# Four RWKV pairs in one tick: corrections and outputs share one PSUM bank, state products have another

## The chip, the cores and the metric

The kernel runs on one core of one Trainium2 chip. The metric is device microseconds (us) for one launch, taken as the median over runs. An engine is one of PE (matmul), DVE (vector), ACT (scalar), POOL (GpSimd) and SP (which issues most DMAs); each works through its own queue in order.

## The reference

One hybrid layer is computed for 256 context tokens and 1024 latent tokens. A combined input projection feeds a differential attention (8 heads) and a bidirectional RWKV-7 recurrence (16 heads of size 64), and an output projection joins both. What the change touches is the recurrence, the attention that is woven into it, and the order of both:

```python
def step(S, inp):                       # rwkv_scan, per token, per head, two directions
    r_t, w_t, k_t, v_t, kk_t, b_t = inp
    sa = jnp.einsum('bhvk,bhk->bhv', S, -kk_t)
    S = S * w_t[:, :, None, :] + sa[..., None] * b_t[:, :, None, :] + v_t[..., None] * k_t[:, :, None, :]
    return S, jnp.einsum('bhvk,bhk->bhv', S, r_t)
...
s = jnp.einsum('bqhmd,bkhmd->bhmqk', qblk, k).astype(F32) * scale      # diff_attention, per 128 queries
p = jax.nn.softmax(s, axis=-1)
a = p[:, :, 0] - lam * p[:, :, 1]
return jnp.einsum('bhqk,bkhv->bqhv', a.astype(v.dtype), v)
```

## The kernel before

The first stage (to about 1249 us) is the input projection and the preparation of the recurrence's operands in DRAM. The second stage, `mix_phase`, runs the recurrence, the attention, the norms and most of the output projection together. The rest is a tail with the last attention blocks and the last set of the output projection.

**The recurrence.** Heads come in pairs; four pairs (`NL = 4`) go side by side as two "duos" (`w` 0 and 1, `e` the pair in it, `h` the head, `d` the direction). Tokens are cut into segments of 256 and chunks of 32. An item is one segment of one group of four pairs; there are ten items (`m`), five for each group. A **tick** (`t`, 80 in all, eight to an item) is one chunk, and `step` writes its work out. In a tick PE makes 16 small matmuls of *corrections* (line 893), which ACT copies out for duo 0 and DVE for duo 1 (line 901, four copies each) into rows 96:128 of the operand tile `R`. Then come 16 matmuls of *state products* (line 913), which DVE multiplies by decays into the next chunk's `R` (line 924, four operations), and 16 matmuls of *outputs* (line 936), which ACT copies to `ys` (line 939, one copy for each duo). `L` and `R` have two slots for each duo, one for a "part" of two chunks; `load_part` fetches the part after next, and `prep` (line 803) multiplies it by the inverse.

**PSUM.** `bank[w]` holds all three products of duo `w`: corrections in columns 0:128, outputs in 128:256, state products in 256:512. All instructions that touch one such tile are ordered by the framework by its bank, not by its columns.

**The attention.** `attention()` is a generator of 80 blocks of 128 queries: scores (`sc`, line 1057, two PSUM buffers), their eviction with a running minimum (line 1060, DVE), exponentials (line 1068, ACT), the combination of both maps (line 1081, DVE), transposes (`pa`, line 1089, copied by ACT in line 1091) and values (`po`, line 1104). `fill` is called twice in a tick, once between corrections and state products and once after the outputs. It adds to a `credit` and draws pieces of attention until that is spent: 1.06 of an even share in the first 40 ticks, 0.68 in the others. What is left goes to the tail. `fill` also moves on the norms of finished items (line 980 and after), the output projection (lines 1255 on) and `invert`.

**The inverse.** For each item but the first, POOL computes 128 triangular 32x32 inverses in 31 steps (two operations each, lines 734 and 736). 16 DMAs bring the matrices (`aw`, line 726), one takes the result to DRAM (line 738), and `load_inv` fetches it for each part. `invert(m + 1)` is begun in the first tick of item `m`, and moved on by eight steps in a tick.

**What sets the order.** PE's queue is the order in which the program is written. On the other engines a list scheduler with a modelled timeline places the instructions; `ahead(500)` around lines 901 and 924 raises their priority.

Of the kernel before, what the change touches and what calls it, by code (L numbers as in the profile page):

```python
# [10 lines left out]
F32 = mybir.dt.float32  # L11
# [7 lines left out]
P = 128  # L19
# [13 lines left out]
CH = 32  # L33
SEG = 256
NC = SEG // CH
HN = 2
NF = NC // HN
NL = 4
# [702 lines left out]
def mix_phase(ctx, tc, i, o, s, ident, nhalf, dram, td0, neglam, subg, lnh, heads, psm):  # L741
    nc = tc.nc
# [85 lines left out]
    def invert(b):  # L828
        rows = inv_rows(heads, b)
        aw = wk.tile([P, CH, CH], F32, tag="aw", name=f"aw{b}")  # L830
        tt = wk.tile([P, CH, CH], F32, tag="tt", name=f"tt{b}")
        tmp = wk.tile([P, CH * CH // 4], F32, tag="tmp", name=f"tmp{b}")
        tds[b] = dram.tile([CH, P, CH], F32, tag=f"td{b % 2}", name=f"td{b}")
        yield from inverse(nc, s, tds[b], rows, aw, tt, tmp)

    bank = [psx.tile([P, 512], F32, name=f"bank{w}") for w in duos]
    yb = psx.tile([P, 512], F32, name="yb")
    sts, wcs = {}, {}

# [15 lines left out]
    def start_item(w, m):  # L855
        p0, sg = items[m]
        R = slots[w, 0][1]
        if sg == -1:
            nc.gpsimd.memset(R[0:64, 0], 0.0)
        if sg != 0:  # L860
            return
        px = bank[w]
        turned = lambda v: v.rearrange("p (d v) -> p d v", d=2)
        for e in range(2):
            p = p0 + 2 * w + e
            for g in range(4):
                c = slice(64 * (g % 2), 64 * (g % 2) + 64)
                nc.tensor.transpose(px[0:64, 64 * g:64 * g + 64], R[0:64, 0, g // 2, e, c], ident[0:64, 0:64])
                nc.tensor.transpose(px[0:64, 256 + 64 * g:256 + 64 * g + 64], sts[p][:, g // 2, c], ident[0:64, 0:64])
            nc.scalar.copy(R[0:64, 0, :, e], turned(px[0:64, 256:512]))  # L870
            fo = wk.tile([HD, 2, P], F32, tag="st", name=f"fo{p}", bufs=NL)
            nc.scalar.copy(fo, turned(px[0:64, 0:256]))
            for d in range(2):
                nc.sync.dma_start(o["new_s"][0, 0, d, 2 * p:2 * p + 2].rearrange("h v k -> v h k"),
                                  fo[:, d, :].rearrange("v (h k) -> v h k", h=2))

    ysb = {}
# [4 lines left out]
    def step(j, k, fill):  # L882
        m, f = j // NF, j % NF
        c = HN * f + k
        p0, sg = items[m]
        hv = lambda h: slice(64 * h, 64 * h + 64)
        for w in duos:
            L, R = slots[w, j % 2]
            for d in range(2):
                for e in range(2):  # L890
                    for h in range(2):
                        u = 64 * e + 32 * h
                        nc.tensor.matmul(bank[w][u:u + 32, 64 * d:64 * d + 64], L[0:96, e, h, d, k, 96:128],
                                         R[0:96, k, d, e, hv(h)], start=True, stop=True, tile_position=(0, u))
        with ahead(HPC):
            for w in duos:
                R = slots[w, j % 2][1]
                for e in range(2):
                    for h in range(2):
                        u = 64 * e + 32 * h  # L900
                        (nc.vector.tensor_copy if w else nc.scalar.copy)(
                            R[96:128, k, :, e, hv(h)], bank[w][u:u + 32, 0:128].rearrange("p (d v) -> p d v", d=2))
        later_prep = k == HN - 1 and j + 1 < n_part
        if later_prep:
            prep(j + 1, 0, yb)
        fill(0)
        for w in duos:
            L, R = slots[w, j % 2]
            for e in range(2):
                for d in range(2):  # L910
                    for h in range(2):
                        o_ = 256 + 128 * d + 64 * e
                        nc.tensor.matmul(bank[w][hv(h), o_:o_ + 64], L[:, e, h, d, k, 0:64],  # L913
                                         R[:, k, d, e, hv(h)], start=True, stop=True, tile_position=(0, 64 * h))
        with ahead(HPC):
            for w in duos:
                if k < HN - 1:
                    dst = slots[w, j % 2][1][0:64, k + 1]
                elif f == NF - 1 and sg == 3:
                    continue  # L920
                else:
                    dst = slots[w, (j + 1) % 2][1][0:64, 0]
                for h in range(2):
                    nc.vector.tensor_tensor(dst[:, :, :, hv(h)], bank[w][hv(h), 256:512].rearrange("p (d e v) -> p d e v", e=2, d=2),  # L924
                                            wcs[p0][hv(h), 2 * w:2 * w + 2, sg + 1, :, c:c + 1].rearrange("p e d o -> p d e o").broadcast_to([HD, 2, 2, HD]), op=ALU.mult)
        g = c // 4
        if c % 4 == 0:
            ysb[m, g] = cp.tile([P, 4, NL, HD], F32, tag="ys", name=f"ys{m}_{g}", bufs=YBUF)
        for w in duos:
            L, R = slots[w, j % 2]  # L930
            for e in range(2):
                o_ = P + 64 * e
                for h in range(2):
                    for d in range(2):
                        q = 64 * d + 32 * h
                        nc.tensor.matmul(bank[w][q:q + 32, o_:o_ + 64], L[:, e, h, d, k, 64:96], R[:, k, d, e, hv(h)],  # L936
                                         start=True, stop=True, tile_position=(0, q))
        for w in duos:
            nc.scalar.copy(ysb[m, g][:, c % 4, 2 * w:2 * w + 2], bank[w][:, P:2 * P].rearrange("p (e v) -> p e v", e=2))  # L939
        if later_prep:  # L940
            prep(j + 1, 1, yb)
        fill(1)
# [463 lines left out]
    def fill(pos):  # L1406
        for _ in range(2):
            state["credit"] += total / (4 * n_tick) * RATES[2 * state["t"] // n_tick]
            while state["credit"] > 0 and state["n"] < heads * NT - NT + 6:
                r = next(att, None)  # L1410
                if r is None:
                    break
                turn(outs)
                state["credit"] -= r
            if state["inv"] is not None:
                for _ in range(2):
                    next(state["inv"], None)
            turn(norms)
            turn(norms, 1)
            turn(projs)  # L1420

    for t in range(n_tick):
        m, c = t // NC, t % NC
        p0, sg = items[m]
# [4 lines left out]
        if c == 0:  # L1429
            for w in duos:  # L1430
                start_item(w, m)
            if m + 1 < n_item:
                state["inv"] = invert(m + 1)
            if sg == 2 and m + 2 < n_item:
                load_pairs(m + 2)
        if 1 <= j and j + 1 < n_part:
# [112 lines left out]
```

## Time and profile before

| | |
|---|---|
| median of 3 runs | 2735.05 us (2734.28 to 2735.93) |
| the profiled execution: its own time, its span | 2740.22 us, 2738.4 us |
| busy in the span: PE, DVE, ACT, POOL | 84%, 57%, 44%, 43% |
| mean granted TensorE clock | 0.927 of full |
| chain that ended last, by engine | PE 47%, DMA 17%, DVE 14%, POOL 7%, ACT 7%, SPq 5%, issue 4% |
| DMA | 437.56 MB, mean 160 GB/s; hardware queue busy 63.6% of 16 engines' span |

The span runs from the first to the last instruction, and the execution's own time has 1.8 us around it. Busy shares are averages over stages that are limited by different things, so the stretch of the 80 ticks is read by itself. The wait lists say for which instruction an idle engine waited; a chain of waits shows which of these ended last.

### The profile page before, as it was taken

The numbers are of one execution on the slowest core, as the hardware profiler recorded it, in microseconds if no ns is written. First come the engines' busy times: TensorE is split into PE (matmuls) and PEld (weight loads), VectorE is DVE, ScalarE is ACT, GpSimd is POOL, SyncE is SP. The second block draws the span as 40 slices with busy tenths as digits, with TensorE's granted clock in tenths as the row PEclk, the third lists the DMA queues.
The fourth block names the chain that finished last, engine by engine and source line by source line (L and its number), as shares of the span: only waits on it lengthen the run. The fifth ranks groups of instructions, "written<-read, shape, count | busy, mean of one in ns | idle before, by whom it ended". The sixth has DMA issues, their size and how long they took to land.

```text
span 2738.4 us, 60831 instructions
## 1 busy us (share of the span) xinstructions
PE 2308.9 (84%) x23907; PEld 1899.5 (69%) x23907; DVE 1564.8 (57%) x3210; ACT 1202.9 (44%) x2606; POOL 1181.5 (43%) x1725
## 2 busy tenths in 40 slices
PE   6999999999999999985778877476778787977786
PEld 4788888888878888774666666365666676765664
DVE  5656565555556564333667666376545555656548
ACT  3334333343434343313666666364545554553332
POOL 4243343342524334472666774575412311133454
PEclk9999999999999999997889998788888999989889
DMA  7465656466555645669687878658675886786435
GB/s 229 117 156 143 170 143 186 129 170 159 129 154 143 170 129 148 164 157 223 139 173 147 177 139 167 102 127 166 158 183 137 185 190 169 188 196 210 129 114 174
DMA packets 516733, 437.56 MB, mean 160 GB/s; under 512 B 156551, under 2 KB 460851, under 8 KB 511328
## 3 DMA queue, kind: packets, MB, share of 16 engines
q1 hardware_dynamic: 514352, 427.94, 63.6%
q0 software_dynamic: 2096, 5.75, 1.2%
q8 instruction: 188, 3.08, 0.5%
q14 instruction: 97, 0.79, 0.1%
HBM read 258.69 MB, written 163.86 MB: 154 GB/s over the span
## 4 chain that ended last, share of the span: by engine, by line
PE 47%; DMA 17%; DVE 14%; POOL 7%; ACT 7%; SPq 5%; issue 4%; DVEq 0%; POOLq 0%; ACTq 0%
PE sc L1057 4%; PE po L1104 4%; DVE R L924 4%; PE pg L449 2%; PE pa L1089 2%; DVE pb L1081 2%; ACT pb L1068 2%; PE pso L1298 2%; PE pso L1300 2%; PE pso L1299 2%; PE yb L803 2%; DVE pb L1060 2%; ACT L L806 1%; DMA acc<-acc 1%; PE ptk L453 1%
## 5 line engine op out<-in xcount | busy, mean ns | idle before, releaser
L1057 PE MATMUL sc<-ka,q 128*128 128x512 f32 (+1 forms) x832 | 313.0, 467 | 61.4 <-DVE pb L1060 36.8
L1060 DVE TENSOR_SCALAR_CACHE_REDUCE pb<-sc,mn 128x512 f32<-128x512 f32 x256 | 191.9, 750 | 145.1 <-PE sc L1057 137.2
L1068 ACT ACTIVATE pb<-pb,mn 128x1536 f32<-128x1536 f32 (+1 forms) x160 | 218.3, 1365 | 117.1 <-DVE pb L1060 116.0
L1104 PEld LDWEIGHTS po<-vk,aT 128*128 128x128 f32 x1600 | 224.9, 207 | 24.0 <-ACT aT L1091 6.2
L1104 PE MATMUL po<-vk,aT 128*128 128x128 f32 x1600 | 233.0, 293 | 4.1 <-ACT aT L1091 4.1
L734 POOL TENSOR_TENSOR tmp<-aw,tt 128x31 f32<-128x31 f32 (+15 forms) x310 | 164.2, 530 | 157.3 <-DMA aw<-kt 55.5
L936 PE MATMUL bank<-R,L 128*32 128x64 f32 x2560 | 74.1, 239 | 168.2 <-DVE R L924 168.0
L479 POOL TENSOR_SCALAR ta<-ta,ka 128x256 f32<-128x256 f32 x80 | 87.2, 1090 | 296.6 <-DVE bk L477 296.5
L1057 PEld LDWEIGHTS sc<-ka,q 128*128 128x128 f32 x832 | 142.8, 211 | 93.4 <-DVE pb L1060 53.4
L456 ACT COPY km<-ptk 64x256 f32<-64x256 f32 x320 | 117.6, 367 | 191.6 <-PE ptk L453 165.4
L736 POOL TENSOR_TENSOR tt<-tt,tmp 128x31 f32<-128x31 f32 (+15 forms) x310 | 184.3, 594 | 21.2
L936 PEld LDWEIGHTS bank<-R,L 128*32 128x32 f32 x2560 | 46.5, 116 | 192.7 <-DVE R L924 192.5
L1089 PE MATMUL pa<-ident,pb 128*128 128x128 f32 x800 | 139.6, 301 | 43.8 <-DVE pb L1081 15.8
L1081 DVE SCALAR_TENSOR_TENSOR pb<-pb,cc,pb 128x512 f32<-128x512 f32 (+1 forms) x208 | 170.3, 868 | 2.5
L1089 PEld LDWEIGHTS pa<-ident,pb 128*128 128x128 f32 x800 | 105.2, 154 | 79.5 <-issue 21.8
L450 DVE TENSOR_TENSOR km<-pg,msk 128x512 f32<-128x512 f32 x80 | 55.1, 688 | 182.3 <-PE pg L449 163.2
L806 ACT COPY L<-yb 32x384 f32<-32x384 f32 x312 | 146.6, 470 | 26.7 <-PE yb L803 23.0
L1060 DVE TENSOR_SCALAR_CACHE_REDUCE pb<-sc 128x512 f32<-128x512 f32 (+1 forms) x160 | 101.7, 637 | 87.4 <-PE sc L1057 84.4
L924 DVE TENSOR_TENSOR R<-bank,wc 64x256 f32<-64x256 f32 x312 | 131.2, 421 | 31.5 <-PE bank L913 23.1
L1091 ACT COPY aT<-pa 128x512 f32<-128x512 f32 (+1 forms) x208 | 115.7, 568 | 74.2 <-PE pa L1089 72.4
L1282 POOL TENSOR_TENSOR olo<-of,ohi 128x512 fp32r<-128x512 f32 x30 | 40.3, 1344 | 214.2 <-ACT ohi L1281 200.9
L939 ACT COPY ys<-bank 128x128 f32<-128x128 f32 x160 | 41.5, 265 | 199.3 <-PE bank L936 183.7
(354 smaller groups left out, 6589.3 us busy)
## 6 DMA issues: line engine op xcount, KB each, us to landing
kt<-km SPq DMA_DIRECT2D x160, 256.0 KB
L<-kt SPq DMA_DIRECT2D x80, 512.0 KB
acc<-acc SPq DMA_DIRECT2D x50, 512.0 KB
ra<-ra SPq DMA_DIRECT2D x160, 128.0 KB
L<-ra SPq DMA_DIRECT2D x80, 256.0 KB
R<-vb SPq DMA_DIRECT2D x160, 64.0 KB
y<-ys SPq DMA_DIRECT2D x80, 128.0 KB
yn<-y SPq DMA_DIRECT2D x40, 256.0 KB
```

Of the source, the lines that this page charges most:

```text
L456: nc.scalar.copy(km[64 * h:64 * h + 64, e:NC:2, 0:HD], pt[64 * e:64 * e + 64, :, 64 * h:64 * h + 64])
L734: e.tensor_tensor(mv, aw[:n, t, t + 1:CH].unsqueeze(2).broadcast_to([n, w, j]), tt[:n, t:t + 1, 0:j].broadcast_to([n, w, j]), op=ALU.mult)
L736: e.tensor_tensor(tt[:n, t + 1:CH, 0:j], tt[:n, t + 1:CH, 0:j], mv, op=ALU.add)
L806: nc.scalar.copy(L[96:128, :, q // 2, q % 2, :, 0:96], pp[32 * q:32 * q + 32, 0:192 * HN].rearrange("p (e c y) -> p e c y", e=2, y=96))
L924: nc.vector.tensor_tensor(dst[:, :, :, hv(h)], bank[w][hv(h), 256:512].rearrange("p (d e v) -> p d e v", e=2, d=2), wcs[p0][hv(h), 2 * w:2 ...
L936: nc.tensor.matmul(bank[w][q:q + 32, o_:o_ + 64], L[:, e, h, d, k, 64:96], R[:, k, d, e, hv(h)], start=True, stop=True, tile_position=(0, q))
L1057: nc.tensor.matmul(sc, q[:, v, m, qc], ka[:, m, 0:kn], start=(v == 0), stop=(v == 1))
L1060: nc.vector.tensor_scalar(pm[:, c * 512:c * 512 + kn], sc, -0.125, mn[:, c - 1:c] if c else None, op0=ALU.mult, op1=ALU.min, accum_out=mn[ ...
L1068: nc.scalar.activation(v, v, AF.Exp, bias=mn[:, c:c + 1], scale=-1.0, accum_out=B["l"][:, m, B["b"]:B["b"] + 1])
L1081: nc.vector.scalar_tensor_tensor(a, B["p"][1][:, v], B["cc"], a, op0=ALU.mult, op1=ALU.add)
L1089: nc.tensor.transpose(pt[:, t * P:(t + 1) * P], B["p"][0][:, 512 * c + t * P:512 * c + (t + 1) * P], ident)
L1104: nc.tensor.matmul(po, B["aT"][c][:, t * P:(t + 1) * P], vk[:, t, :], start=(c == 0 and t == 0), stop=(c == last and t == nt - 1))
```

## The change

Both duos' corrections go to one bank (`bank[0]`, columns 0:256) and so do both duos' outputs (256:512); both duos' state products go to the other (`bank[1]`, duo `w` in 256w:256w+256). One ACT copy of 128x256 takes the outputs of both. The item start's transposes, which had a bank for each duo, all use `bank[1]`. The inverses of all items become one sequence that is moved on in proportion to the ticks (33 calls for 8 ticks, four ticks ahead of the item) in place of eight steps a tick from the item's first tick on. The attention's credit starts at minus two ticks' even share.

```diff
+INVA = 4
+LEAD = 2
...
-    bank = [psx.tile([P, 512], F32, name=f"bank{w}") for w in duos]
+    bank = [psx.tile([P, 512], F32, name=f"bank{n}") for n in range(2)]
...
-        px = bank[w]
+        px = bank[1]
...
-                        nc.tensor.matmul(bank[w][u:u + 32, 64 * d:64 * d + 64], L[0:96, e, h, d, k, 96:128],
+                        nc.tensor.matmul(bank[0][u:u + 32, P * w + 64 * d:P * w + 64 * d + 64], L[0:96, e, h, d, k, 96:128],
...
-                            R[96:128, k, :, e, hv(h)], bank[w][u:u + 32, 0:128].rearrange("p (d v) -> p d v", d=2))
+                            R[96:128, k, :, e, hv(h)], bank[0][u:u + 32, P * w:P * w + P].rearrange("p (d v) -> p d v", d=2))
...
-                        o_ = 256 + 128 * d + 64 * e
-                        nc.tensor.matmul(bank[w][hv(h), o_:o_ + 64], L[:, e, h, d, k, 0:64],
+                        o_ = 256 * w + 128 * d + 64 * e
+                        nc.tensor.matmul(bank[1][hv(h), o_:o_ + 64], L[:, e, h, d, k, 0:64],
...
-                o_ = P + 64 * e
+                o_ = 256 + P * w + 64 * e
...
-                        nc.tensor.matmul(bank[w][q:q + 32, o_:o_ + 64], L[:, e, h, d, k, 64:96], R[:, k, d, e, hv(h)],
+                        nc.tensor.matmul(bank[0][q:q + 32, o_:o_ + 64], L[:, e, h, d, k, 64:96], R[:, k, d, e, hv(h)],
...
-        for w in duos:
-            nc.scalar.copy(ysb[m, g][:, c % 4, 2 * w:2 * w + 2], bank[w][:, P:2 * P].rearrange("p (e v) -> p e v", e=2))
+        nc.scalar.copy(ysb[m, g][:, c % 4], bank[0][:, 256:512].rearrange("p (x v) -> p x v", x=NL))
...
-            if state["inv"] is not None:
-                for _ in range(2):
-                    next(state["inv"], None)
+            while state["ninv"] < 33 * (state["t"] + INVA + _ / 4 + pos / 2) / NC:
+                next(state["inv"], None)
+                state["ninv"] += 1
...
+    def inverses():
+        for b in range(1, n_item):
+            yield from invert(b)
+            yield
+
+    state["inv"], state["ninv"] = inverses(), 0
+    state["credit"] = -LEAD * total / n_tick
...
-            if m + 1 < n_item:
-                state["inv"] = invert(m + 1)
```

Line numbers of the changed kernel are two higher up to the outputs' copy and one higher after it. How instructions move is shown at three places. In the names, `R0x` and `L0x` are duo 0's tiles and `R1x` and `L1x` duo 1's; what stands behind "waits" are the engines or DMA queues on whose counters the instruction waits.

PE, tick 12, from the state products to the first attention piece after the outputs. Before:

```order
L913 MATMUL bank0_12282<-R00_11564,L00_11563 64x64 x8
L913 MATMUL bank1_12283<-R10_11584,L10_11583 64x64 x8
L936 MATMUL bank0_12282<-R00_11564,L00_11563 32x64 [waits DVE_49]
L936 MATMUL bank0_12282<-R00_11564,L00_11563 32x64 x7
L936 MATMUL bank1_12283<-R10_11584,L10_11583 32x64 [waits DVE_49]
L936 MATMUL bank1_12283<-R10_11584,L10_11583 32x64 x7
L1104 MATMUL po1_2_14675<-vk_1_0_12584,aT1_2_0_14601 128x128 x4
```

The same place with the change:

```order
L915 MATMUL bank1_12283<-R10_11584,L10_11583 64x64 [waits DVE_49] x2
L915 MATMUL bank1_12283<-R10_11584,L10_11583 64x64 x2
L915 MATMUL bank1_12283<-R10_11584,L10_11583 64x64 [waits DVE_49] x2
L915 MATMUL bank1_12283<-R10_11584,L10_11583 64x64 x2
L938 MATMUL bank0_12282<-R00_11564,L00_11563 32x64 x8
L938 MATMUL bank0_12282<-R10_11584,L10_11583 32x64 x8
L1058 MATMUL sc1_2_0_1_14558<-ka_1_1_13948,q_1_0_13322 128x512 x2
```

The outputs' wait for DVE is gone: 156 of the output matmuls of before wait for DVE, none of the change's does.

DVE, tick 12, from the last score eviction ahead of duo 1's copies to the state updates. Before:

```order
L1060 TENSOR_SCALAR pb1_12288,mn1_3_14503<-sc1_3_0_1_14519,mn1_3_14503 128x512 [waits DVE_49,PE_49]
L901 COPY R10_11584<-bank1_12283 32x2x64 [waits PE_49,Activation_49]
L901 COPY R10_11584<-bank1_12283 32x2x64 x3
L1060 TENSOR_SCALAR pb1_12288,mn1_3_14503<-sc1_3_0_2_14591,mn1_3_14503 128x512 [waits DVE_49,PE_49]
L1060 TENSOR_SCALAR pb2_12289,mn1_3_14503<-sc1_3_1_0_14603 128x512 [waits PE_49]
L1060 TENSOR_SCALAR pb2_12289,mn1_3_14503<-sc1_3_1_1_14615,mn1_3_14503 128x512 [waits DVE_49,PE_49]
L1060 TENSOR_SCALAR pb2_12289,mn1_3_14503<-sc1_3_1_2_14626,mn1_3_14503 128x512 [waits DVE_49,PE_49]
L924 TENSOR_TENSOR R00_11564<-bank0_12282,wc0_12310 64x4x64 [waits PE_49,Activation_49]
```

The same place with the change:

```order
L1061 TENSOR_SCALAR pb2_12289,mn1_1_14268<-sc1_1_1_2_14465,mn1_1_14268 128x512 [waits DVE_49,PE_49]
L903 COPY R10_11584<-bank0_12282 32x2x64 [waits Activation_49]
L903 COPY R10_11584<-bank0_12282 32x2x64 x3
L1061 TENSOR_SCALAR pb0_12287,mn1_2_14481<-sc1_2_0_0_14488 128x512 [waits PE_49]
L1075 RECIPROCAL cc1_1_14269<-l1_0_14167 128x1 [waits Activation_49]
L1076 SCALAR_TENSOR_TENSOR cc1_1_14269<-cc1_1_14269,l1_0_14167,neglam_82 128x1 [waits DVE_49]
L1082 SCALAR_TENSOR_TENSOR pb1_12288<-pb2_12289,cc1_1_14269,pb1_12288 128x512 [waits DVE_49]
L1082 SCALAR_TENSOR_TENSOR pb1_12288<-pb2_12289,cc1_1_14269,pb1_12288 128x512 x2
L926 TENSOR_TENSOR R00_11564<-bank1_12283,wc0_12310 64x4x64 [waits PE_49]
```

In all 80 ticks duo 1's copies on DVE now wait for the last of duo 0's four copies on ACT, which read the same bank; before, 62 of them named ACT, for the output copy of the tick before. The attention pieces beside them are also about two blocks earlier ones.

POOL, where the norms of an early segment (`yn0_2`, line 980, 981 with the change) meet an inverse. Before:

```order
L738 DMA td7_21109<-tt7_21107 128x32x32 [waits DMASW3_49,Pool_49]
L1137 TENSOR_SCALAR f3_3_18199<-f3_3_18199 128x4 [waits Pool_49]
L729 MEMSET tt8_22619 128x1024 [waits DMASW3_49]
L730 MEMSET tt8_22619 128x32 [waits Pool_49]
L734 TENSOR_TENSOR tmp8_22620<-aw8_22618,tt8_22619 128x31 [waits DMAHW4_49,DMAHW3_49,DMAHW5_49,DMAHW2_49,DMAHW6_49,DMAHW1_49,DMAHW7_49,DMAHW0_49,Pool_49]
L736 TENSOR_TENSOR tt8_22619<-tt8_22619,tmp8_22620 128x31 [waits Pool_49]
L734 TENSOR_TENSOR tmp8_22620<-aw8_22618,tt8_22619 128x60 [waits Pool_49]
L980 TENSOR_TENSOR yn0_2_18488<-yn0_2_18488 128x2x256 [waits DMAHW2_49,DVE_49]
```

With the change:

```order
L736 TENSOR_TENSOR tmp7_20225<-aw7_20223,tt7_20224 128x256 [waits Pool_49]
L738 TENSOR_TENSOR tt7_20224<-tt7_20224,tmp7_20225 128x16x16 [waits Pool_49]
L736 TENSOR_TENSOR tmp7_20225<-aw7_20223,tt7_20224 128x255 [waits Pool_49]
L738 TENSOR_TENSOR tt7_20224<-tt7_20224,tmp7_20225 128x15x17 [waits Pool_49]
L736 TENSOR_TENSOR tmp7_20225<-aw7_20223,tt7_20224 128x252 [waits Pool_49]
L738 TENSOR_TENSOR tt7_20224<-tt7_20224,tmp7_20225 128x14x18 [waits Pool_49]
L981 TENSOR_TENSOR yn0_2_18328<-yn0_2_18328 128x2x256 [waits DMAHW5_49,DVE_49]
L736 TENSOR_TENSOR tmp7_20225<-aw7_20223,tt7_20224 128x247 [waits Pool_49]
```

The norm's addition stood behind the first step of the eighth inverse, the one that waits for the DMAs of `aw`; now it stands behind the 18th step of the seventh. Both orders run all nine inverses one after the other, far ahead of the items that need them.

## Rows read from the trace of the kernel before

**Rows 1.** Windows: 40 ticks, 40 ticks, tail; columns as in the first line
```profile
core 0: us, PE busy (x) PEld busy (x) DVE busy (x) ACT busy (x) POOL busy (x), PEclk, DMA share, GB/s
1309.00:1904.00 595.00, 436.93 (x6611) 353.83 (x6610) 384.86 (x968) 335.56 (x793) 382.87 (x703) 0.87 0.76 149
1904.00:2491.00 587.00, 481.29 (x6793) 386.46 (x6792) 330.60 (x829) 305.68 (x731) 156.51 (x247) 0.90 0.73 174
2491.00:2738.00 247.00, 181.61 (x856) 142.18 (x856) 151.28 (x302) 80.68 (x170) 120.40 (x156) 0.88 0.48 156
```
**Rows 2.** PE's waits, 1249 to 2491 us: us in total, times, longest us
```profile
PE bank L936 <- DVE R L924: 168.0, 154, 29.9
PE sc L1057 <- DVE pb L1060: 35.1, 22, 9.1
PE sc L1057 <- DMA ka<-klo: 24.1, 3, 21.9
...
PE bank L913 <- DVE R L901: 6.0, 2, 4.8
...
PE bank L868 <- ACT fo L872: 4.0, 4, 1.2
```
**Rows 3.** Timeline of PE in tick 12: start us, us, what [idle before]
```profile
1466.28 1.15 PE L913 MATMUL bank<-R,L 128*64 128x64 f32 x32
1467.99 0.43 PE L936 MATMUL bank<-R,L 128*32 128x64 f32 x16 [0.56 <-DVE R L924]
1468.88 0.43 PE L936 MATMUL bank<-R,L 128*32 128x64 f32 x16 [0.46 <-DVE R L924]
```
**Rows 4.** Timeline of DVE in tick 12: duo 1's copies, the state updates
```profile
1462.67 1.20 DVE L901 COPY R<-bank 32x128 f32<-32x128 f32 x4
...
1467.08 1.74 DVE L924 TENSOR_TENSOR R<-bank,wc 64x256 f32<-64x256 f32 x4
```
**Rows 5.** Window of 20 us that holds tick 12, columns as in rows 1
```profile
1460.00:1480.00 20.00, 17.32 (x284) 13.86 (x282) 17.90 (x44) 13.85 (x33) 18.09 (x28) 1.00 0.81 162
```
**Rows 6.** Timeline of ACT in tick 12: duo 0's copies, an exponential
```profile
1461.97 1.06 ACT L901 COPY R<-bank 32x128 f32<-32x128 f32 x4
...
1464.69 1.58 ACT L1068 ACTIVATE pb<-pb,mn 128x1536 f32<-128x1536 f32 x1 [1.05 <-DVE pb L1060]
```
**Rows 7.** Groups by line, 1249 to 2491 us: busy us, mean ns | idle before
```profile
L924 DVE TENSOR_TENSOR R<-bank,wc 64x256 f32<-64x256 f32 x312 | 131.2, 421 | 31.5 <-PE bank L913 23.1 <-ACT ob L1110 2.1 <-ACT L L806 0.8
...
L939 ACT COPY ys<-bank 128x128 f32<-128x128 f32 x158 | 41.1, 265 | 199.3 <-PE bank L936 183.7 <-DMA y<-ys 13.1 <-DMA R<-vb 1.4
```
**Rows 8.** Timeline of PE in tick 32
```profile
1780.93 0.65 PE L936 MATMUL bank<-R,L 128*32 128x64 f32 x16 [29.94 <-DVE R L924]
1784.86 0.65 PE L936 MATMUL bank<-R,L 128*32 128x64 f32 x16 [3.28 <-DVE R L924]
```
**Rows 9.** Timeline of DVE in tick 32
```profile
1778.35 0.69 DVE L983 TENSOR_REDUCE m<-yn 128x8 f32<-128x512 f32 x1 [28.59 <-POOL yn L980]
```
**Rows 10.** Timeline of POOL in tick 32
```profile
1753.20 0.95 POOL L729 MEMSET tt<- 128x1024 f32 x1 [6.86 <-DMA td<-tt]
...
1776.14 0.24 POOL L734 TENSOR_TENSOR tmp<-aw,tt 128x31 f32<-128x31 f32 x1 [21.77 <-DMA aw<-kt]
...
1777.05 1.26 POOL L980 TENSOR_TENSOR yn<-yn 128x512 f32<-128x512 f32 x1
```
**Rows 11.** Timeline of PE: corrections of tick 0, first scores, corrections of tick 2
```profile
1249.54 0.65 PE L893 MATMUL bank<-R,L 96*32 96x64 f32 x32
1272.07 1.19 PE L1057 MATMUL sc<-ka,q 128*128 128x512 f32 x2 [21.87 <-DMA ka<-klo]
...
1308.95 0.65 PE L893 MATMUL bank<-R,L 96*32 96x64 f32 x32
```
**Rows 12.** The page's groups: the attention's matmuls on PE, whole span
```profile
L1057 PE MATMUL sc<-ka,q 128*128 128x512 f32 (+1 forms) x832 | 313.0, 467 | 61.4 <-DVE pb L1060 36.8
...
L1104 PE MATMUL po<-vk,aT 128*128 128x128 f32 x1600 | 233.0, 293 | 4.1 <-ACT aT L1091 4.1
...
L1089 PE MATMUL pa<-ident,pb 128*128 128x128 f32 x800 | 139.6, 301 | 43.8 <-DVE pb L1081 15.8
```
**Rows 13.** DVE's waits, 1249 to 2491 us: us in total, times, longest us
```profile
DVE pb L1060 <- PE sc L1057: 211.2, 165, 21.6
```

More of the change, by code (lines that the diff above doesn't have):

```diff
@@ L923, in step @@
                 for h in range(2):
-                    nc.vector.tensor_tensor(dst[:, :, :, hv(h)], bank[w][hv(h), 256:512].rearrange("p (d e v) -> p d e v", e=2, d=2),
+                    nc.vector.tensor_tensor(dst[:, :, :, hv(h)], bank[1][hv(h), 256 * w:256 * w + 256].rearrange("p (d e v) -> p d e v", e=2, d=2),
                                             wcs[p0][hv(h), 2 * w:2 * w + 2, sg + 1, :, c:c + 1].rearrange("p e d o -> p d e o").broadcast_to([HD, 2, 2, HD]), op=ALU.mult)
```

## The prediction

> **What bounds the kernel now.** I read the windows first, because busy shares over the whole span mix stages. In the first 40 ticks PE is busy 436.93 of 595 us (73%), DVE 65%, POOL 64%; in the next 40 PE 481.29 of 587 us (82%), DVE 56% [rows 1]. No engine is full, so the ticks are held by waits, and PE is nearest to full. Next come PE's waits [rows 2]: outputs (L936) waiting for the state updates on DVE (L924) make up 168.0 us in 154 waits, more than all others together. The timeline of a usual tick shows why: state products are issued at 1466.28 and take 1.15 us, each duo's outputs then stand 0.56 and 0.46 us [rows 3], while DVE's four updates run from 1467.08 for 1.74 us [rows 4]. An update writes slot k+1 of `R`; an output matmul reads slot k. They share no data, only the bank: the update reads columns 256:512 of the bank into which the outputs write columns 128:256. The change takes that away, and in the order none of its output matmuls waits for DVE any more.
>
> The longest of these waits has another origin. In tick 32 PE stands 29.94 + 3.28 = 33.2 us [rows 8], since DVE stands 28.59 us at L983 for a norm's sum of POOL [rows 9], which stands behind an inverse step that waited 21.77 us for its DMAs [rows 10].
>
> **Part by part**, against the profiled execution's 2740.2 us.
>
> *Outputs no longer wait.* 78 ticks update a state (the last tick of each group does not). At 0.56 + 0.46 = 1.02 us [rows 3] the regular wait is 79.6 us. Behind the outputs stand attention matmuls that can run while DVE updates; but each update that is late also holds the evictions behind it, and scores already wait 35.1 us for those [rows 2]. I take 0.8 of it as recovered: **−64** (bounds 0 and −80). Of the rest, 168.0 − 79.6 − 33.2 = 55 us are ticks where DVE came late, with evictions ahead of the updates. That lateness stays; PE goes on with attention until both score buffers are full or the next corrections need `R`. A score matmul costs with all that follows it 685.6 us / 832 = 0.82 us of PE (313.0 + 233.0 + 139.6 [rows 12]), so some pieces suffice to cover one such wait, but not a long one. I take 0.4: **−22** (bounds 0 and −55).
>
> *Tick 32.* In the new order the norm's sum stands behind the 18th step of the seventh inverse, not behind the first of the eighth, and the reduction on DVE stands behind the updates. PE's outputs would not wait there in any case, but its scores wait for DVE if a norm still stalls it elsewhere. I take **−20** (bounds 0 and −33).
>
> *Copies in series.* All four copies of duo 1 on DVE (1.20 us [rows 4]) now wait for all four of duo 0 on ACT (1.06 us [rows 6]): in tick 12 they began 0.7 us apart and lay side by side. State products of duo 1 then come up to 1.06 us later, and wait for the copies one by one. In that tick there were 2.4 us between the copies' end (1462.67 + 1.20 = 1463.87) and the state products (1466.28), and over all ticks the state products waited only 6.0 us, in 2 waits [rows 2], so most ticks have the slack, thanks to the attention in between. DVE stands meanwhile, though, in its own queue: evictions and updates behind these copies come later. DVE is 90% busy in the 20 us around tick 12 (17.90 of 20 [rows 5]), 56 to 65% over the stage. Bounds: 0, and 80 × 1.06 = 85 us. I take a third, by the stage's shares rather than that window: **+27**.
>
> The trace has this wait for 2 ticks in 80. The Trainium skill, "PSUM — Partial Sum Buffer", section "PSUM bank collisions raise a hardware error", has two engines kept apart on one bank and quadrant, two readers included; a merged bank would by that cost up to 1.06 us each time. With +85 in place of +27 the sum would be −26, about 2709 us; with 0, −111, about 2624. The row on the state products' waits (6.0 us) speaks for the lower half.
>
> *One output copy in place of two.* 158 copies of 265 ns [rows 7] become 79 of double width. ACT is busy 56% (335.56 of 595 [rows 1]): **0**; if ACT bound the stage it would be a gain of up to 41.1/2 = 20 us. *Item start:* the transposes of both duos use one bank, and waited 4.0 us before [rows 2]: **+3** (bounds 0 and +8, three times 4.0 in all). *The inverses:* the order of POOL still runs them one after another far ahead; paced calls alone do not space them. Apart from tick 32, **0**, with ±15 for other norms that move with it: DVE waited at L983 for POOL in other places too.
>
> *Two ticks' start.* At tick 2 the attention has issued 0 scores in place of 27 (order), after the last tick's corrections 735 in place of 755. In the trace, tick 0's corrections run at 1249.54, PE then stands 21.87 us for `ka` until 1272.07, and tick 2 begins at 1308.95 [rows 11]. Without attention a tick is a chain of corrections 0.65, copies 1.06 and 1.20, state products 1.15 and updates 1.74, together 5.8 us [rows 3, 4, 6, 11], and I estimate 6 to 7 us with handovers; two fit into the time in which PE stood. Tick 2 would begin between 1269 and 1282: **−30** (bounds −27 and −40). It comes back at the end: 20 scores × 0.82 us = 16.4 us of PE's work is done in the tail, where PE is busy 181.61 of 247 us (0.735 [rows 1]): **+22** (bounds 0, where the tail's gaps take them, and +27, the whole saving).
>
> Sum: −64 − 22 − 20 + 27 + 0 + 3 − 30 + 22 = −84, so 2656 us for this execution. The median of the runs before, 2735.05, is 5.2 below the profiled execution, so I predict **2651 us**, 3.1% faster.
>
> **Rivals.**
>
> 1. *DVE becomes the bound.* PE no longer waits at the outputs but a little later, at scores, for evictions behind the same late updates. For: the 90% of [rows 5]; 35.1 us of such waits already. Against: DVE itself stood 211.2 us for PE's scores [rows 13], more than PE for DVE. Then half of the regular waits comes back (−40 for −64), nothing of the late ones, half of tick 32 (−10), and the copies cost +35: −40 − 10 + 35 + 3 − 8 = −20, thus about **2715**. Chance 0.17.
>
> 2. *Slower: DVE's queue is blocked at L903.* DVE works in order; when it comes to duo 1's copies, it must wait until ACT has got through its own queue: an exponential of 1.58 us [rows 6] if one is under way, and four copies of 1.06. That is up to 2.64 us a tick, 80 × 2.64 = 211 us of DVE; before, the two copied at the same time. If seven tenths of it reach the path, that is +148, against gains of 64 + 22 + 20 + 8 = 114 and +3 at the item start: +37, thus about **2772**. It decides where DVE is the limiter in more than half of the ticks (114 − 3 = 111 of 211). For: DVE is 90% busy in [rows 5], and the new order puts the copies behind ACT in all 80 ticks. Against: DVE's 211.2 us of idle time at scores [rows 13], in which such a wait disappears, and ACT's 56%. Chance 0.11.
>
> 3. *All recovered.* The 168.0 us go whole, the copies hide in the slack of 2.4 us, the start gives −30 and the tail hides half of its work (+11): −168 + 3 − 30 + 11 = −184 at most; with a tenth of the waits returning as waits for scores, −167, about **2570**. For: the second half already runs PE at 82%. Against: it would need PE busy about 80% throughout with DVE never late. Chance 0.10.
>
> 4. *It doesn't do what it says.* The inverse's steps are not spread in the order. A DMA that comes late then still stalls POOL and, through a norm, DVE, as in tick 32. That alone gives the −20 back, and lies within the forecast's range (2671).
>
> By the Trainium skill, "Perfetto Trace Analysis", section "Optimizing Tensor Performance", independent groups of matmuls should rotate through banks so that evacuating one lies beside the next group's matmuls; the change does so between state products and outputs and gives it up between the duos. The trace prices the first at 168.0 us of waits and the second at 6.0, which is why the forecast goes with the first.
>
> **How the numbers follow.** Forecast 0.62, rivals 0.17, 0.11 and 0.10. The forecast's own range, with the terms' bounds not all at one end, is about 2610 to 2695. To reach 8 in 10 I add rival 1 (2715 and a little above) and the nearer part of rival 3: **2590 to 2725**. About 0.2% (5.5 us) is what a measurement of this kernel can tell from no change. Faster: the forecast whole, rival 3 whole, most of rival 1 (0.13): 0.85. Same: the upper end of rival 1, 0.04. Slower: 0.11.
>
> **What would show it.** Right: no wait of outputs for the state updates in PE's list; scores waiting longer for evictions than 35.1 us, but by less than 100; tick 2's corrections at about 1270 to 1282; the tail about 20 us longer than 247; no wait over 20 us in tick 32. DVE's copies should show waits for ACT of about 1 us in many ticks, while the state products' wait for them stays below 30 us. Wrong: a state products' wait for the copies above 80 us, or a chain of waits with DVE's share far above its 14%, gives rivals 1 and 2; PE's busy share above 85% in both halves gives rival 3; a tick that stands tens of us for a norm elsewhere takes the −20 away.

## The result and the profile after

The changed kernel takes 2616.88 us (median of 4 runs, 2608.0 to 2619.78) against 2735.49 for the kernel before beside it: ratio 0.9556, 95% interval 0.9528 to 0.9585, so 118.6 us or 4.4% faster. The forecast was 2651 us with 2590 to 2725 as its range: the direction was right, the gain was 84 in the forecast and is 119. The profiled execution took 2608.0 us (span 2606.2), at the fast end of the runs; beside the profiled execution of before the span is 132.2 us shorter. A trace shows one execution: over all comparisons below, single runs of the kernel before lie between 2722.68 and 2745.47 us and their medians between 2732.52 and 2735.81, so times are compared by medians, and stretches of two traces only roughly.

The windows of the changed kernel, from tick 2 to tick 40, from there to the end of tick 79, and the tail; columns as in [rows 1]:

```profile
1265.00:1822.00 557.00, 445.30 (x6630) 360.51 (x6626) 387.55 (x979) 333.52 (x758) 379.15 (x696) 0.87 0.82 167
1822.00:2351.00 529.00, 469.95 (x6784) 381.43 (x6772) 324.06 (x825) 297.84 (x680) 165.04 (x268) 0.93 0.83 192
2351.00:2606.00 255.00, 190.79 (x930) 150.60 (x930) 158.46 (x335) 95.29 (x199) 123.29 (x168) 0.89 0.51 164
```

PE's busy share rises from 73% to 80% (445.30 of 557) in the first half of the ticks and from 82% to 89% (469.95 of 529) in the second. Its idle time in both halves was 595 − 436.93 + 587 − 481.29 = 263.8 us [rows 1] and is 557 − 445.30 + 529 − 469.95 = 170.7 us: 93 us less. Its busy time hardly moved (918.2 and 915.3 us).

PE's waits from tick 0 to the end of tick 79 (us in total, times, longest us), the view of [rows 2]:

```profile
PE sc L1058 <- DVE pb L1061: 61.1, 32, 8.4
PE pa L1090 <- DVE pb L1082: 15.7, 15, 3.6
PE yb L805 <- DMA Tb<-td: 11.7, 3, 7.0
PE sc L1058 <- DMA ka<-klo: 8.9, 3, 7.6
PE bank L915 <- DVE R L903: 8.2, 5, 3.9
PE bank L870 <- ACT fo L874: 7.3, 6, 3.3
```

The outputs' line (L938) no longer stands there: 168.0 us [rows 2] are gone. A part comes back, first of all in the first row: scores wait 61.1 us for evictions, 35.1 before. Transposes waiting for the combination (15.7) stood at 7.6 us, in a row of before that I had not shown:

```profile
PE pa L1089 <- DVE pb L1081: 7.6, 6, 2.5
```

From tick 2 on, the outputs had waited 160.7 us. Of these 93 are won, and PE's other idle time grew by 68 us: 28 at scores, 8 at transposes, the rest in many small rows.

DVE's waits in the same stretch:

```profile
DVE pb L1061 <- PE sc L1058: 101.5, 98, 9.4
DVE R L903 <- ACT R L903: 92.1, 45, 9.7
...
DVE m L984 <- POOL yn L981: 37.2, 10, 11.0
```

DVE stood 211.2 us for scores [rows 13] and now 101.5; in addition it stands 92.1 us at duo 1's copies, for ACT's. All its idle time in the two windows of the ticks fell from 466.5 to 374.4 us.

Timeline of PE in tick 12, from the state products on (start us, us, what, idle before):

```profile
1429.40 1.15 PE L915 MATMUL bank<-R,L 128*64 128x64 f32 x32
1430.48 0.65 PE L938 MATMUL bank<-R,L 128*32 128x64 f32 x32
1431.07 0.74 PE L1058 MATMUL sc<-ka,q 128*128 128x512 f32 x2
...
1435.48 0.74 PE L1058 MATMUL sc<-ka,q 128*128 128x512 f32 x2 [1.88 <-DVE pb L1061]
1436.90 0.65 PE L895 MATMUL bank<-R,L 96*32 96x64 f32 x32 [0.68 <-ACT ys L940]
```

and of DVE in the same tick:

```profile
1428.25 1.25 DVE L903 COPY R<-bank 32x128 f32<-32x128 f32 x4 [0.22 <-ACT R L903]
...
1430.88 2.11 DVE L1082 SCALAR_TENSOR_TENSOR pb<-pb,cc,pb 128x512 f32<-128x512 f32 x3
1432.91 1.72 DVE L926 TENSOR_TENSOR R<-bank,wc 64x256 f32<-64x256 f32 x4
```

All 16 output matmuls (the trace has two records for each) follow the state products in 0.65 us, where before they came in two halves with 0.56 and 0.46 us of waiting [rows 3]. The updates begin at 1432.91, 1.8 us after the outputs were done: under the old layout the outputs of a duo stood behind its updates. PE does attention instead, and meets a wait of 1.88 us at the next score, for an eviction that stands behind those updates: the return that the forecast allowed for. The wait of 0.68 us at the next corrections is for the output copy, which reads the bank into which they write. That order was there before the change, too; such waits were 0.8 us in the 80 ticks and are 6.3 now.

The start, timeline of PE:

```profile
1238.84 0.65 PE L895 MATMUL bank<-R,L 96*32 96x64 f32 x32 [0.43 <-issue]
1246.14 1.11 PE L895 MATMUL bank<-R,L 96*32 96x64 f32 x18 [3.13 <-DVE R L926]
...
1261.40 1.19 PE L1058 MATMUL sc<-ka,q 128*128 128x512 f32 x2 [7.57 <-DMA ka<-klo]
...
1264.84 1.08 PE L895 MATMUL bank<-R,L 96*32 96x64 f32 x32
```

Tick 0 takes 7.3 us (1238.84 to 1246.14; I had estimated 6 to 7), PE's wait for the first keys is 7.57 us in place of 21.87 [rows 11], and tick 2 begins at 1264.84. The forecast had 1269 to 1282 for it; tick 0 itself began 10.7 us earlier than in the trace of before.

The span's 132.2 us by stretch, from the corrections' starts in both traces (tick 0, 2, 79, end: 1249.54, 1308.95, 2483.16, 2738.45 before; 1238.84, 1264.84, 2343.84, 2606.22 after):

| stretch | before | after | difference | terms of the forecast |
|---|---|---|---|---|
| until tick 0 | 1249.5 | 1238.8 | −10.7 | none |
| ticks 0 and 1 | 59.4 | 26.0 | −33.4 | −30 |
| ticks 2 to 78 | 1174.2 | 1079.0 | −95.2 | −64 − 22 − 20 + 27 + 3 = −76 |
| tick 79 and the tail | 255.3 | 262.4 | +7.1 | +22 |

I don't put the first row down to the change: in the runs below tick 0 begins anywhere from 1236.5 to 1246.9 us, also where the banks are those of before.

### The profile page after: what moved, and what is told of

The parts are those of the page before. It is cut to its first block, busy times and chain, and to the rows that moved or that the text cites. A ratio compares the mean times of both kernels' runs of the same rounds, so it can differ in the third digit from the quotient of the medians.

```text
span 2606.2 us, 60633 instructions
## 1 busy us (share of the span) xinstructions
PE 2295.6 (88%) x23907; PEld 1895.5 (73%) x23907; DVE 1547.9 (59%) x3210; ACT 1194.9 (46%) x2530; POOL 1172.6 (45%) x1725
## 4 chain that ended last, share of the span: by engine, by line
PE 47%; DMA 18%; DVE 11%; POOL 9%; SPq 5%; ACT 5%; issue 4%; POOLq 0%; DVEq 0%; ACTq 0%
PE sc L1058 3%; PE pg L451 3%; DVE pb L1082 2%; PE po L1105 2%; DMA wst<-w_out 2%; PE bank L915 2%; DVE pb L1061 2%; PE pso L1299 2%; PE pa L1090 2%; DMA acc<-acc 2%; PE pso L1301 1%; PE ptk L455 1%; PE pso L1300 1%; DMA yn<-y 1%; DVE R L926 1%
## 5 line engine op out<-in xcount | busy, mean ns | idle before, releaser
L1105 PEld LDWEIGHTS po<-vk,aT 128*128 128x128 f32 x1600 | 216.2, 200 | 23.9 <-ACT ob L1111 3.3
L1105 PE MATMUL po<-vk,aT 128*128 128x128 f32 x1600 | 225.4, 286 | 4.1 <-ACT ob L1111 2.0
L903 DVE COPY R<-bank 32x128 f32<-32x128 f32 x320 | 92.6, 289 | 103.3 <-ACT R L903 92.1
L1299 PE MATMUL pso<-wohi,ohi 128*128 128x512 f32 x240 | 104.5, 435 | 30.7 <-ACT ohi L1282 17.3
L915 PEld LDWEIGHTS bank<-R,L 128*64 128x64 f32 x2560 | 95.9, 145 | 35.5 <-issue 12.2
```

Of the source, the lines that this page charges most:

```text
L915: nc.tensor.matmul(bank[1][hv(h), o_:o_ + 64], L[:, e, h, d, k, 0:64], R[:, k, d, e, hv(h)], start=True, stop=True, tile_position=(0, 64 * h))
L1105: nc.tensor.matmul(po, B["aT"][c][:, t * P:(t + 1) * P], vk[:, t, :], start=(c == 0 and t == 0), stop=(c == last and t == nt - 1))
L1299: nc.tensor.matmul(ps, ohi[:, k - k0, :], whi[:, k, c], start=(n == 0), stop=False)
```

## The experiments

My theory after this: the banks alone bring nearly all, the late attention a little, the inverse's pacing nothing. Rivals: the pacing took away the stall of tick 32 (33.2 us), or the late attention carries a third. Then the one cost that I had booked, copies in series, was tested from several sides. Every ratio is to the kernel before, run beside it on the same chip.

**The three edits one at a time.** `e1_banks` is the kernel before with the new layout and the single output copy only.

> The banks alone (the kernel before with only the new PSUM layout and the single output copy). Theory: the outputs' wait for the state updates, 168.0 us before, is what the change saves, and PE gets back 90 to 110 us of it: 2625 to 2645 us, and the list of PE's waits shows no wait of outputs for DVE. Rival: a third or more of the change's 118 us comes from the inverse's pacing and from the late attention: 2655 to 2690 us.

Measured: 2631.57 us, ratio 0.9638 (0.9613 to 0.9662), so about 99 us of the 118.6, as the theory had it. (The single output copy was not tested apart; ACT's time for output copies in the ticks is 41.1 us before and 29.1 with the change.) No wait of outputs for DVE is left; scores wait 61.3 us:

```profile
PE sc L1058 <- DVE pb L1061: 61.3, 41, 9.7
PE sc L1058 <- DMA ka<-klo: 23.3, 3, 21.0
```

`e2_lead` is the kernel before with one line, put ahead of the loop over ticks:

```diff
+    state["credit"] = -LEAD * total / n_tick
```

> The attention's late start alone, on the kernel before. Theory: the first two ticks run while PE would stand for the first keys, and a part comes back in the tail: 8 to 34 us faster, 2701 to 2727 us; tick 2 begins at 1265 to 1285 us. Rival: the attention is only put off, and the tail takes back all that the start gives: 2730 to 2740 us.

Measured: 2705.95 us, ratio 0.9903 (0.988 to 0.9925), 27 us. Tick 2 begins at 1266.3 us. PE's outputs wait less as well, which I had not expected:

```profile
PE bank L937 <- DVE R L925: 125.8, 155, 5.2
PE sc L1058 <- DVE pb L1061: 24.4, 20, 11.9
```

The longest is 5.2 us in place of 29.9 [rows 2]: with the attention two ticks later the stall of tick 32 does not come about in this run. So the 27 us are not the start alone.

`e3_inv` is the kernel before with the changed kernel's `inverses()` and its pacing.

> The inverse's pacing alone, on the kernel before. Theory: the stall of 33.2 us in tick 32 goes or shrinks, since the norm's sum no longer stands behind the inverse step that waits for its matrices: 2700 to 2722 us. Rival 1: the order of POOL moves and the stall turns up at another norm: 2730 to 2740 us. Rival 2: the steps collide with norms elsewhere, and it is slower by 5 to 15 us.

Measured: 2735.56 us, ratio 1.0008 (0.9992 to 1.0024). The theory failed: the stall is still there, in tick 32; timelines of SP, POOL, DVE and PE of this run:

```profile
1764.20 1.88 SPq L972 DMA_DIRECT2D yn<-y  x3
...
1769.33 0.24 POOL L735 TENSOR_TENSOR tmp<-aw,tt 128x31 f32<-128x31 f32 x1 [19.86 <-DMA aw<-kt]
...
1771.53 0.69 DVE L984 TENSOR_REDUCE m<-yn 128x8 f32<-128x512 f32 x1 [27.42 <-POOL yn L981]
...
1774.11 0.66 PE L937 MATMUL bank<-R,L 128*32 128x64 f32 x16 [28.77 <-DVE R L925]
```

The first row shows what the prediction had not looked at. The norm's sum on POOL (L981) needs `yn`, and SP issues the loads of `yn` only at 1764.20; by the trace's semaphore record the first of them, the last that this sum needed, landed at 1769.74, and the sum ran at 1770.24. In the kernel before it is the same:

```profile
1771.43 1.88 SPq L971 DMA_DIRECT2D yn<-y  x3
```

This load landed at 1776.59, and the sum ran at 1777.05 [rows 10]. So the sum could have run at most 0.5 us earlier without the inverse step ahead of it. DVE, in its turn, stood at the reduction that needs this sum, with the state updates behind it. The pacing moves POOL's steps, not this load, and it is not what takes the stall out of the changed kernel's path.

`e4_no_lead` is the changed kernel without the line of the late start.

```diff
-    state["credit"] = -LEAD * total / n_tick
```

> The changed kernel with the attention's credit started at zero again. Theory: the late start is worth the 44 us by which tick 2 begins earlier, less the 10 us by which the tail is longer: 2640 to 2655 us. Rival: it is worth what I had in the sum, 8 us (30 at the start, 22 back in the tail): 2620 to 2630 us. If it is worth nothing, 2612 to 2620 us.

Measured: 2628.97 us, ratio 0.9618 (0.9593 to 0.9643). The late start is worth 12 us by the medians, 17 by the ratios (0.9618 − 0.9556), nearer to the 8 of my sum, the rival of this run, than to the 34 of its theory. In its trace tick 2 begins at 1303.9 (1264.8 with the late start: −39, of which 3.5 us before tick 0), ticks 2 to 78 take 1069.5 (1079.0: +9.5), tick 79 and the tail 255.3 (262.4: +7.1). Of the 35.6 us won in ticks 0 and 1, 16.6 are lost again, about half of them in the later ticks and half in the tail.

`e5_no_inv` is the changed kernel with the inverses begun and stepped as before.

> The changed kernel with the inverses begun and paced as before (banks and late attention alone). Theory (the pacing gives nothing, as on the kernel before): 2612 to 2625 us. Rival (with the attention late, steps that are begun four ticks ahead keep POOL out of the norms' way, or the rearranged order of itself is worth more than the pacing): 2630 to 2645 us, as in the two controls, where a small edit of the preparation cost 24 us.

Measured: 2612.94 us, ratio 0.9561 (0.9548 to 0.9574): the pacing brings nothing here either.

**The copies in series.** `e7_corr_apart` puts duo 1's corrections into the 128 columns of `yb` that the preparation of the next part does not use:

```diff
+    cor = [bank[0][:, 0:P], yb[:, 3 * P:4 * P]]
...
-        if later_prep:
-            prep(j + 1, 0, yb)
         fill(0)
+        if later_prep:
+            prep(j + 1, 0, yb)
```

> The changed kernel with the corrections' copies side by side again: duo 1's corrections go to the 128 columns of another bank that the preparation of the next part leaves free (that preparation is moved behind the first fill, so that it does not wait for the copies). DVE's copies then no longer wait for ACT's, a wait that takes 90.7 us of DVE in the changed kernel. Theory of my sum: the series costs about 27 us, so 2580 to 2600 us. Rival: DVE's wait is hidden, since PE's state products wait only 8.2 us for the copies: 2607 to 2622 us. Rival 2: the new bank brings waits of PE for the preparation: above 2622 us.

`e9_prep_late` is its control, with the second hunk alone.

> Control for the run with the corrections apart: the changed kernel with nothing but the first half of the preparation moved behind the first fill. Expected by all: within 6 us of the changed kernel, 2610 to 2625 us.

Measured: 2617.06 us (0.956, 0.9535 to 0.9584) with the corrections apart, and 2640.98 (0.9649, 0.9624 to 0.9673) in the control. With the corrections apart the time is in the first rival's range, not in that of my sum. The pair differs by 24 us, but the control was slower than expected: the late preparation itself costs 24 us over the changed kernel, and its lists of PE's and of DVE's waits show what moved:

```profile
PE sc L1058 <- DVE pb L1061: 44.7, 34, 8.3
PE yb L805 <- ACT L L808: 34.9, 30, 3.3
...
DVE R L903 <- ACT R L903: 38.2, 32, 8.9
```

The second half of the preparation now waits for ACT to have copied the first; the changed kernel has no such wait. In this control the series takes only 38.2 us of DVE, so it is a poor measure of the 92.1 us in the changed kernel; and of the 24.5 us between the two profiled executions 9.3 lie ahead of tick 0, where the corrections play no part. So I moved the first half back and gave it another bank. `e10_corr_pt` has the corrections apart with

```diff
-            prep(j + 1, 0, yb)
+            prep(j + 1, 0, pst.tile([P, 512], F32, tag="pt", name=f"pp{j}"))
```

> The corrections apart, without the late preparation: duo 1's corrections in the free columns of the preparation's bank, the first half of the preparation where it was in the program, in one of the two rotating banks that the attention's transposes use. Theory (the series of copies costs about 24 us, the difference between the run with the corrections apart and its control): 2585 to 2600 us. Rival (the 24 us were won only because the late preparation had made the copies' wait worse, and with the preparation in place the wait is hidden): 2610 to 2622 us.

and `e11_prep_pt` this hunk alone.

> Control for the run before it: the changed kernel with nothing but the first half of the preparation in one of the transposes' banks. Expected if the banks of the transposes have room: within 6 us of the changed kernel, 2610 to 2624 us; if the transposes wait for it: 2624 to 2640 us. What the corrections' series costs is read as the difference to this run.

Measured: 2616.91 us (0.9579, 0.9556 to 0.9602; again the rival's range) and 2641.26 (0.9658, 0.963 to 0.9686; its six runs lie between 2637.05 and 2644.51 but for one of 2621.95). Again the pair differs by 22 to 24 us, and again the control is 24 us slower than the changed kernel. In the first of them DVE's wait for ACT is gone, but DVE waits 47.0 us at the same copies for PE's corrections, and PE's scores wait 43.6 us. The control's DVE waits as the changed kernel's does, and its transposes wait for the bank that the preparation has taken from them, as the second expectation had it:

```profile
DVE pb L1061 <- PE sc L1058: 129.8, 114, 11.4
DVE R L903 <- ACT R L903: 95.8, 47, 8.9
...
PE pa L1090 <- ACT L L808: 17.7, 8, 7.2
```

So with the preparation in another place or bank, taking the copies apart wins 22 to 24 us. Beside the changed kernel itself neither arrangement with the copies apart is faster (2617.06 and 2616.91 against 2616.88); whether the series costs it anything, and the other edits use up what is won, stays open. Another way was not tried: the four copies of each engine lie in four different groups of 32 partitions, and an order by partitions would put each copy of DVE behind one copy of ACT, not behind all four. No run shows what that would do.

**The copies on one engine.** `e6_act_copies` and `e8_dve_copies` are the changed kernel with all eight copies on ACT, or on DVE:

```diff
-                        (nc.vector.tensor_copy if w else nc.scalar.copy)(
+                        nc.scalar.copy(
```

> The changed kernel with all eight copies of corrections on ACT: DVE loses 92.6 us of work and the 90.7 us in which it waits for ACT, ACT gains about 85 us (320 copies of 265 ns). Theory (DVE's lateness is what holds the scores, 61.1 us of PE's waits): 10 to 40 us faster than the changed kernel, 2575 to 2607 us. Rival: DVE has time to spare, and ACT's longer queue brings exponentials and copies late: 2615 to 2640 us.

> The changed kernel with all eight copies on DVE: DVE gains 92 us of work and loses the wait for ACT. Theory (DVE's queue is what PE waits for next): 20 to 70 us slower than the changed kernel, 2637 to 2687 us. Rival (only the wait between the engines costs, not DVE's work): 2605 to 2620 us.

Measured: 2631.03 us on ACT (0.96, 0.9575 to 0.9626) and 2645.95 on DVE (0.9664, 0.964 to 0.9687). The first is in its rival's range, the second in its theory's. About 90 us less work on DVE bring nothing, about as much more costs 29 us. The first of these does not show that DVE has time to spare, since ACT has some 80 us more to do. With the copies on ACT the scores wait less, but PE waits for ACT's other copies:

```profile
PE sc L1058 <- DVE pb L1061: 43.4, 27, 9.7
...
PE pa L1090 <- ACT aT L1092: 15.8, 13, 8.2
PE yb L805 <- ACT L L808: 13.3, 9, 5.6
```

**A longer start.** `e12_lead4` is the changed kernel with `LEAD = 4`.

> The changed kernel with the attention begun four ticks later in place of two. Theory (what is won at the start is the time in which PE stood for the first keys, 21.0 us, and two ticks fill it; what is put off beyond that runs in the tail at its lower share): 3 to 15 us slower than the changed kernel, 2620 to 2632 us. Rival (each tick without attention runs the recurrence ahead for nothing more): 2600 to 2612 us.

Measured: 2652.19 us, ratio 0.9697 (0.9673 to 0.9722), 35 us slower, more than I expected. The recurrence runs into its own operands: PE stands 26.0 us in tick 3 for `Tb`, the inverse of the next part. Its load is issued at 1282.25, behind the keys and queries of the attention (rows of PE, then of SP):

```profile
1258.37 1.08 PE L895 MATMUL bank<-R,L 96*32 96x64 f32 x32
1265.07 1.08 PE L895 MATMUL bank<-R,L 96*32 96x64 f32 x32 [0.49 <-ACT ys L940]
1292.18 1.50 PE L805 MATMUL yb<-L,Tb 32*32 32x96 f32 x32 [26.02 <-DMA Tb<-td]
...
1282.25 0.59 SPq L795 DMA_DIRECT2D Tb<-td  x1
```

This wait uses up most of what the longer start wins, but it is not the loss itself: from tick 0 to tick 4 this run still takes 7.6 us less than the changed kernel (56.8 and 64.3 us). Ticks 4 to 78 then take 33.2 us more (1073.8 and 1040.7), and tick 79 and the tail 19.0 more (281.4 and 262.4). Why the later ticks are that much longer is not shown. No run is clearly faster than the changed kernel.

## Why the prediction was right, and where its sizes were off

**What the outputs' wait was: right.** The prediction read 168.0 us as a wait for a bank alone, and the layout with its single output copy gives 99 us.

**Where the 35 us between forecast and result lie.** The forecast's gain was 84 us, the measured one 118.6. The run with the banks alone stands against five terms, −64 − 22 − 20 + 27 + 3 = −76, and has −99: they were 23 us too small together. The late start stands against −30 + 22 = −8 and has −12 to −17. The pacing stands against 0 and has 0.

**How much of the wait comes back.** The return is where the forecast put it: scores waiting for evictions, 61.1 us for 35.1, with transposes waiting for the combination beside them. The size is not settled: the terms −64, −22 and −20 recover 106 of 168.0 us, and the 23 us are missing there, in the next term, or in the single output copy, which was put at 0.

**Copies in series, +27: perhaps too much, not shown.** The prediction took a third of the upper bound by DVE's busy share. For nearly nothing in its place speaks that PE's state products wait 8.2 us for the copies, 6.0 before [rows 2], and that DVE, which stands 92.1 us for ACT in 45 waits, had stood 211.2 us for scores [rows 13] and stands 101.5 now, so that the wait can lie in time that DVE had. With 0 in place of +27 the sum is −111. For +27 speaks that the pairs of runs differ by 22 to 24 us; but in one control the series took only 38.2 us of DVE, and in the runs with the copies apart DVE stood 41.7 and 47.0 us at them all the same, for PE. If the series does cost that much, it was the 106 us that were set too low. The figure of up to 1.06 us for each wait, besides, belongs to the order by whole banks that the framework keeps; by groups of 32 partitions, I estimate, it would be about one of the four copies, 1.06/4 = 0.27 us.

**Tick 32, −20: the stall went, but its cause was misread.** The prediction put it down to the inverse step ahead of the norm's sum. The sum's own operand landed only 0.5 us before it ran, so the inverse's place on POOL was worth no more than that; with the pacing alone the stall of 28.77 us stays. It goes with the banks alone, where PE has no wait of that length but the one for the first keys, and with the late start alone. DVE's longest wait for a norm's sum is 28.6 us before, 27.4 with the pacing, 13.5 with the banks, 12.3 with the late start and 11.0 with all three. Why these two orders avoid it is not shown, so it is luck that the term came true. The order on POOL that I had shown as the change's effect is an effect of the whole new schedule, not of the pacing. That the inverse's spread does nothing by itself (rival 4) holds on both kernels; that the −20 would then be lost does not hold.

**The two ticks' start: −30 right, +22 too much.** Ticks 0 and 1 are 33.4 us shorter. In the tail 7 us came back, not 22: 18 scores more are left for it (718 issued by tick 79 in place of 736), and PE's busy share there rises from 0.735 to 0.75. But the runs with and without the late start show another 9.5 us in the ticks between. Together 12 to 17 us are won where the sum had 8.

**The rivals.** DVE as the bound (1): PE's wait at scores for evictions grew as described, by 26 us, but the run with less work on DVE is not faster. Slower by DVE's blocked queue (2): the blocking is there, 92.1 us rather than 211, and the kernel is faster all the same. All recovered (3): PE's share passed 85% in the second half only.

## What to carry to other kernels

A wait for a tile need not be a wait for data: where the waiting and the awaited instruction use different columns of one PSUM bank, the list of waits prices a new layout, and here some 60% of that wait was won. A part of the rest returns at the next things that the late engine owes, here the evictions of scores. What the new order between the copies costs could be read neither from DVE's busy share (+27) nor from PE's wait at the next instruction (8.2 us) with certainty: the tests of it needed other edits, which cost as much as they were to measure. A stall is followed back through every operand of the instruction that came late: here a norm stood behind an inverse step and behind its own load, and moving the step could not help. Putting work off to start the recurrence early paid for two ticks; with four, the recurrence stood 26 us for an operand of its own, and the later ticks and the tail took 52 us more.

## What the runs showed of the hardware that I had not expected

The time reacts to small edits by as much as to the mechanism that is tested: moving half of the preparation behind the first fill, or into another bank, cost 24 us each. Each has waits of its own in PE's list (34.9 us for the first, 17.7 us of transposes for the second), but the runs with the same place or bank and the copies apart have 29.7 and 14.9 us of them and are 24 us faster, so these waits alone don't explain it. With a scheduler that re-orders three engines after each edit, a control with the same small edit is needed beside every experiment, and a difference of 20 us between two single programs says little about the mechanism that was edited. The mean granted clock in the second half of the ticks is 0.93 of full where it was 0.90 [rows 1], with PE busier (89% of the time, 82% before), not idler.
